# Two attention heads normed and turned together, a denser modulation vector and a longer queue of queries and keys

## The chip, the core and the metric

The kernel runs on one core of a Trainium2 chip. TensorE (PE, the matrix engine, with its weight loads shown as PEld), VectorE (DVE), ScalarE (ACT) and GpSimd (POOL) each work through a queue of their own, in order; SyncE (SP) issues most DMAs. Semaphores tie the queues together. The metric is the device time of one execution in microseconds (us); lower is better. Shown are the median of several runs and one execution taken apart by the profiler.

## The reference

One layer: adaptive modulation of a normed input, a projection `w_in`, sparse attention and an RWKV time mix side by side, an output projection, and a gated feed-forward network (FFN), all in float32 on 512 tokens of width 2048.

```python
mod = silu(c) @ w_ada[l] + b_ada[l]
sh1, sc1, gt1, sh2, sc2, gt2 = jnp.split(mod[:, None, :], 6, axis=-1)
h = rms_norm(x, norm1_g[l]) * (1 + sc1) + sh1
proj = h @ w_in[l]                    # q, k, v, iq, ik, iw and the RWKV columns
q = partial_rope(rms_norm(q.reshape(B, S, 8, 128), q_norm_g[l]), positions)
k = partial_rope(rms_norm(k.reshape(B, S, 8, 128), k_norm_g[l]), positions)
att_out = dsa_sparse_attention(q, k, v, iq, ik, iw)   # each query keeps its 128 best keys
rwkv_out = rwkv7_time_mix(rwkv_proj, ...)
x = x + gt1 * (jnp.concatenate([att_out, rwkv_out], axis=-1) @ w_out[l])
h2 = rms_norm(x, norm2_g[l]) * (1 + sc2) + sh2
x = x + gt2 * ((silu(h2 @ w_ffn_gate[l]) * (h2 @ w_ffn_up[l])) @ w_ffn_down[l])
```

`partial_rope` turns the first 32 of a head's 128 columns. In the kernel a head lies as a tile of 128 columns (partitions) by 512 tokens, so the turned part is its first 32 partitions.

## The kernel before

**Dense work.** All projections are *jobs* of weights: a job is a chunk of four 128-row blocks of a weight matrix times 256 columns. Each float32 operand is split into a high and a low part (`split`: the high part by an ACT cast, `whi`; the low by a DVE subtraction, `wlo`), and each product is three matmuls, so a chunk gives 24 matmuls of 128x128 by 512, and a pair of heads, four chunks, 96. Weights come through four DMA buffers (`wraw`) and four buffers each of `whi` and `wlo`, one for half a chunk. A pair of heads gathers in two of four `pg` banks of PSUM, and `evac_qk` empties them on ACT: for each head `t` (the head times its gain, named `q` or `k` in the trace) and a square `sq`.

**Side work.** Everything else runs as *streams*: Python generators that `drive` steps after every three matmuls (`every=3` in `run_jobs`). The program is written out once, by a planner that keeps a clock for each engine (`clk`, `cost`, `ready`): a stream waits with `until` (its inputs ready by the planner's clock), `room` (DVE's clock at most so far ahead of PE's) and `banks` (a free PSUM bank), and then writes its instructions into the queues between the matmuls. Where a job's `need` is not met, no matmul is written; the planner's clock moves on in steps of 0.25 until it is. On the chip only the order in each queue and the semaphores are left of that.

**Around the change.** The attention jobs come in the order q0 and q1, k0 and k1, q2 and q3, k2 and k3, and so on, each with `need=few`. `qk` holds heads whose `q` or `k` is made and not yet taken by `head`; two `head_stream`s take them once the top-k of the index scores (`idx_stream`: 16 rounds of `max` and `match_replace` on DVE) is done and both RWKV `scan`s are through (`scanned`). `scan` is a chain of eight steps, each of short matmuls (tiles `p`, `po`) with copies between; then `post` norms the RWKV heads (`pm`, `pst`, `prb`, `pgt`). `norm_qk`, one stream for each head, takes the column sums (`colsum`: a DVE transpose into `tr` and a sum into `sums`), turns the head in place (`rope`: a shuffle and three DVE operations on 32 rows, temporary `u`), spreads the sums by short matmuls into `pst`, takes the power -1/2 on POOL into `rr`, and for a key lays it out with four transposes (`prb`) and multiplies (DVE). Most of these tiles, and those of the heads (`lt`, `vh`), of `post` (`bv`, `sq`) and of the modulation vectors (`wad`), come from one pool `gp` of 27 tiles; an instruction that needs a tile waits until one is given back. Among jobs after the q/k groups are the output projection (`wout`, needs the ended heads) and the FFN.

`ada_stream` makes the modulation vectors `gt1`, `sh2`, `sc2`, `gt2`: 64 chunks each, loaded by SP (`wad`, 256 KB) and multiplied and added on DVE, one chunk at a time at a pace of `PACE1`, `PACE`, `PACE2`. `gt2` starts in the FFN; at its end `ada_sum` sums over partitions into `part`, then the short matmuls `pc`. All down projections have `need=lambda: done["ada"] == 16`, that is, `gt2` must be there.

In the profile nearly every instruction has line 127, the planner's helper, so groups are told apart by tile names.

Of the kernel before, what the change touches and what calls it, by code (L numbers as in the profile page):

```python
# [8 lines left out]
F32 = mybir.dt.float32  # L9
F32R = mybir.dt.float32r  # L10
I32 = mybir.dt.int32
AF = mybir.ActivationFunctionType
OP = mybir.AluOpType
# [6 lines left out]
NT = S // 128  # L20
# [6 lines left out]
NORM_EPS = 1e-6  # L27
# [16 lines left out]
C_FQ, C_FI, C_SQ, C_SI, C_HS, C_ONE, C_SEL, C_EXP, C_MOD = 512, 513, 514, 515, 516, 518, 519, 520, 522  # L44
# [4 lines left out]
def layer_kernel(ctx, tc, x, c, positions, w_ada, b_ada, norm1_g, w_in, q_norm_g, k_norm_g,  # L49
# [13 lines left out]
    def nm(ap):  # L63
        t = getattr(ap, "tensor", None)
        return getattr(t, "name", None)
# [22 lines left out]
    class Queue:  # L88
# [3 lines left out]
        def __getattr__(self, op):  # L92
# [3 lines left out]
            def call(*args, **kw):  # L96
# [26 lines left out]
                if key2 != "pe":  # L123
                    for v in vals[1:]:
                        if nm(v) in psread:
# [4 lines left out]
    PE, V, A, P, SP = (Queue(e, k) for e, k in ((nc.tensor, "pe"), (nc.vector, "dve"), (nc.scalar, "act"),  # L130
                                                (nc.gpsimd, "pool"), (nc.sync, "dma")))

    def now():
        return clk["pe"]

    SLACK = 0.5
    PACE1, PACE, PACE2 = 3.6, 1.9, 3.0

    def until(*aps):

        t = max(ready.get(nm(a), 0.0) for a in aps) + SLACK
        while now() < t:
            yield

    def room(key="dve", lim=3.0):
        while clk[key] - now() > lim:
            yield

    def banks(n):

        while True:
            for k in [k for k, v in psread.items() if v is not None and v <= now()]:
                del psread[k]
            if len(psread) + n <= 4 and side["pe"] <= SIDE:
                return
            yield
# [12 lines left out]
    rpool = ctx.enter_context(tc.tile_pool(name="rp", bufs=8))  # L169
# [3 lines left out]
    def G(name="g", dt=F32):  # L173
        return gpool.tile([128, 512], dt, name=name, tag="g")
# [7 lines left out]
    def SM(name="sm"):  # L182
        return spool.tile([128, 16], F32, name=name, tag="sm")
# [4 lines left out]
    def PS(name="ps"):  # L188
        t = psp.tile([128, 512], F32, name=name, tag="ps")
        psread[nm(t)] = None  # L190
        return t

    def mm(o, l, r, start=True, stop=True):
        PE.matmul(o, l, r, start=start, stop=stop)
# [8 lines left out]
    ident = cst[:, C_ID:C_ID + 128]  # L203
# [5 lines left out]
    mhalf = cst[:, C_EXP:C_EXP + 1]  # L209
# [148 lines left out]
    for k1, n1 in BLOCKS:  # L358
        for kind in ("scale", "shift"):
            n = 4 // n1  # L360
# [56 lines left out]
    ps = PS()  # L417
# [18 lines left out]
    att = {}  # L436
# [88 lines left out]
    def colsum(dst, t):  # L525

        u = G("tr")
        V.transpose(u, t)
        V.tensor_reduce(dst, u.rearrange("p (b c) -> p b c", c=32), axis=mybir.AxisListType.X, op=OP.add)

    def spread(ps, parts, col=C_MOD):

        pv = parts.rearrange("p (j a) -> p a j", a=4)
        for a in range(4):
            mm(ps[32 * a:32 * a + 32], cst[:, col:col + 32], pv[:, a, :])
# [294 lines left out]
    scanned = set()  # L830
# [142 lines left out]
    def ada_stream():  # L973
# [15 lines left out]
        for i, (bi, k) in enumerate(chunks):  # L989
            while (bi >= 12 and not state["ffn"]) or (4 <= bi < 12 and len(solved) < 2):  # L990
                yield
            while nl < min(i + 3, 64 if bi < 4 else 192 if bi < 12 else 256):
                load(nl)
                nl += 1
            t = tiles.pop(i)
            while now() < last + (PACE1 if bi < 4 else PACE if bi < 12 else PACE2):
                yield
            yield from until(t)
            yield from room("dve", 0.7 if 4 <= bi and not done["topk"] else 3.5)
            last = now()  # L1000
            if k == 0:
                A.activation(t, t, AF.Copy, scale=ccol(0))
                acc = t
                continue
            V.scalar_tensor_tensor(acc, t, ccol(k), acc, op0=OP.mult, op1=OP.add)
            if k == KD - 1:
                start(ada_sum(acc, *blocks[bi]))

    def ada_sum(acc, n, o, b):
        yield from until(acc)  # L1010
        part = parts[o % 2]
        yield from room("dve", 4.0)
        colsum(part[:, b * 16:b * 16 + 16], acc)
        if b < 3:
            return
        yield from until(part)
        t = now()
        while n == "gt2" and now() < t + 12.0:
            yield
        yield from banks(1)  # L1020
        pc = PS("pc")
        spread(pc[:, 0:16], part)
        yield
        V.tensor_tensor(mod[n], pc[:, 0:16], v1[:, o * 16:o * 16 + 16], op=OP.add)
        if n == "sc2":
            V.scalar_tensor_tensor(gp2, mod[n], 1.0, v1[:, 112:128], op0=OP.add, op1=OP.mult)
        done["ada"] += 4
# [3 lines left out]
    QM = [(i + 16) % 32 for i in range(32)]  # L1031
    IM = [i ^ 8 if i < 16 else i for i in range(32)]

    def rope(t, rows, tab, mask):
        cs, sn = tab
        u = G("u")
        V.stream_shuffle(u[rows], t[rows], mask)
        V.tensor_tensor(u[rows], u[rows], sn[rows], op=OP.mult)
        V.tensor_tensor(t[rows], t[rows], cs[rows], op=OP.mult)
        V.tensor_tensor(t[rows], t[rows], u[rows], op=OP.add)  # L1040
# [91 lines left out]
    head_queue = []  # L1132
    qk = {}
    qstat = {}

    def evac_qk(kind, i0):
        def f(ps):
            gcol = v2[:, R_QN:R_QN + 1] if kind == "q" else v2[:, R_KN:R_KN + 1]
            for i in range(2):
                t, sq = G(kind), G("sq" + kind)  # L1140
                A.activation(t, ps[i], AF.Identity, scale=gcol)
                A.activation(sq, ps[i], AF.Square)
                qk[kind, i0 + i] = t
                start(norm_qk(kind, i0 + i, t, sq))
        return f

    def norm_qk(kind, h, t, sq):
        yield from until(sq)
        yield from room()
        sm = SM("sums")  # L1150
        colsum(sm, sq)
        rope(t, slice(0, 32), att["qtab"], QM)
        yield from until(sm)
        yield from banks(1)
        pst = PS("pst")
        spread(pst[:, 0:4], sm)
        yield
        st, rr = SM("st"), rpool.tile([128, 4], F32, name="rr", tag="rr")
        V.tensor_scalar(st[:, 0:4], pst[:, 0:4], 1.0 / 128, NORM_EPS, op0=OP.mult, op1=OP.add)
        P.tensor_tensor(rr, st[:, 0:4], mhalf.broadcast_to([128, 4]), op=OP.pow)  # L1160
        if kind == "q":
            P.tensor_scalar(rr, rr, 128.0 ** -0.5, 0.0, op0=OP.mult, op1=OP.add)
            qstat[h] = rr
            return
        yield from until(rr)
        yield from banks(1)
        prb = PS("prb")
        for tt in range(NT):
            PE.transpose(prb[:, tt * 128:(tt + 1) * 128], rr[:, tt:tt + 1].broadcast_to([128, 128]), ident)
        yield  # L1170
        V.tensor_tensor(t, t, prb, op=OP.mult)
        head_queue.append(h)


    PLACE = {3: (0, 0), 2: (1, 0), 0: (1, 384), 1: (2, 0)}
# [67 lines left out]
    def start(gen):  # L1243
        streams.append(gen)
# [27 lines left out]
        done["hfree"] += 4  # L1272

    def few():
        return len(qk) <= (6 if len(scanned) == 2 else 4)

    for h in range(0, HEADS, 2):
        group_T(win, h * 128, TWO, ALLK, 4, hrhs, evac_qk("q", h), need=few)
        group_T(win, 1024 + h * 128, TWO, ALLK, 4, hrhs, evac_qk("k", h), need=few, chunk_done=h_free if h == HEADS - 2 else None)
# [253 lines left out]
def constants():  # L1533
    import numpy as np
    t = np.zeros((128, C_W), np.float32)
    p = np.arange(128)
    t[:, C_ID:C_ID + 128] = np.eye(128)
    s, u = p[:, None] % 64, p[None, :] % 64
    t[:, C_MASK:C_MASK + 128] = np.where(p[None, :] < 64, s < u, s <= u)
    t[:, C_CAUS:C_CAUS + 128] = np.where(p[None, :] <= p[:, None], 0.0, FILL)  # L1540
    t[:, C_BLKM:C_BLKM + 128] = (p[:, None] // 64 == p[None, :] // 64) / 64.0
    fq = (np.float32(500000.0) ** (-np.arange(16, dtype=np.float32) / np.float32(16))).astype(np.float32)
    fi = (np.float32(500000.0) ** (-np.arange(8, dtype=np.float32) / np.float32(8))).astype(np.float32)
    t[0:32, C_FQ] = fq[p[:32] % 16]
    r = p % 64
    t[:, C_FI] = np.where(r < 16, fi[p % 8], 0.0)
    t[0:32, C_SQ] = np.where(p[:32] < 16, -1.0, 1.0)
    t[:, C_SI] = np.where(r < 8, -1.0, np.where(r < 16, 1.0, 0.0))
    t[:, C_HS] = p < 64
    t[:, C_HS + 1] = p >= 64  # L1550
    t[:, C_ONE] = 1.0
    t[:, C_SEL] = p % 32 == 0
    t[:, C_EXP] = -0.5
    t[:, C_MOD:C_MOD + 32] = p[:, None] % 32 == np.arange(32)
    t[0:64, C_MOD + 32:C_MOD + 64] = t[0:64, C_MOD:C_MOD + 32]
    t[64:128, C_MOD + 64:C_MOD + 96] = t[64:128, C_MOD:C_MOD + 32]
    return t
# [30 lines left out]
```

## Time and profile before

| | |
|---|---|
| median of three runs | 2716.01 us (2714.59 to 2717.59) |
| the profiled execution | 2714.33 us, of it a span of 2712.5 us from first to last instruction |
| PE busy | 2649.6 us, 98% of the span |
| DVE busy | 1458.6 us, 54% |
| ACT busy | 807.6 us, 30% |
| POOL busy | 181.0 us, 7% |
| granted TensorE clock, mean | 0.987 of full speed |

A view of stretches gives busy time of each engine between two times from the span's start. A view of waits says what ended an engine's idle times. The chain of waits follows the work that ended last back in time. A granted clock of 1.00 is 2.4 GHz, 0.50 is 1.2 GHz; a value between is a mean over a stretch that has both.

### The profile page before, as it was taken

To read this page: it belongs to the slowest core of one execution; us is meant where nothing else is said; L and a number is where in the kernel's file an instruction comes from. 1 tells how busy PE (TensorE), PEld (TensorE's weight loads), DVE (VectorE), ACT (ScalarE), POOL (GpSimd) and SP (SyncE) were. 2 spreads that over 40 slices of the span, in tenths; PEclk is the share of its full clock that TensorE was granted. 3 is DMA by queue.
4 is the path that set the end of the run, shared out by engine and by line. 5 is a ranking of instruction groups with operands and counts; after the bars stand their busy time and mean duration, and the time that the engine had idled before them with its cause. 6 is when DMAs were issued, how large, how long until landed. Compare 5 with 4: busy or idle time off the path is not lost.

```text
span 2712.5 us, 35153 instructions
## 1 busy us (share of the span) xinstructions
PE 2649.6 (98%) x13351; PEld 2102.1 (77%) x13351; DVE 1458.6 (54%) x2542; ACT 807.6 (30%) x1475; POOL 181.0 (7%) x194
## 2 busy tenths in 40 slices
PE   7999999999998999999999899999999999999999
PEld 4477777767776787887888788888888888888887
DVE  3367779979788778755555432323333232332333
ACT  3243333323322334323322222222222222222222
POOL 2001101100021223110000000000000000000000
PEclk8999999999998999999999999999999999999999
DMA  9966675573664344752555232333233332323233
GB/s 323 335 215 194 215 192 179 163 192 115 173 206 126 125 156 144 250 173 64 197 170 177 95 101 94 101 94 97 98 97 98 96 99 95 100 94 101 93 104 98
DMA packets 383802, 396.10 MB, mean 146 GB/s; under 512 B 52538, under 2 KB 332928, under 8 KB 383632
## 3 DMA queue, kind: packets, MB, share of 16 engines
q1 hardware_dynamic: 381392, 387.25, 45.8%
q0 software_dynamic: 2096, 6.34, 0.7%
q8 instruction: 105, 1.72, 0.3%
q14 instruction: 65, 0.53, 0.1%
q10 hardware_dynamic: 144, 0.26, 0.0%
HBM read 358.13 MB, written 35.65 MB: 145 GB/s over the span
## 4 chain that ended last, share of the span: by engine, by line
PE 89%; DVE 5%; issue 2%; DMA 2%; SPq 1%; ACT 1%; POOL 0%; POOLq 0%; DVEq 0%; ACTq 0%
PE acc L127 75%; PE vacc L127 4%; PE p L127 2%; PE po L127 2%; SPq L127 1%; PE adaacc L127 1%; DVE wlo L127 1%; PE dot L127 1%; DVE stmp L127 1%; DMA wada<-in_w_ada_dram 1%; PE pl L127 1%; DVE wad L127 0%; PE pgt L127 0%; DMA xtok<-in_x_dram 0%; DVE X L127 0%
## 5 line engine op out<-in xcount | busy, mean ns | idle before, releaser
L127 DVE TENSOR_TENSOR wlo<-wraw,whi 128x512 fp32r<-128x512 f32 (+2 forms) x868 | 578.8, 673 | 1007.5 <-ACT whi L127 1003.2
L127 PE MATMUL acc<-hhi,whi 128*128 128x512 f32 (+1 forms) x2256 | 908.9, 403 | 6.6 <-ACT hhi L127 6.4
L127 ACT CAST whi<-wraw 128x512 fp32r<-128x512 f32 (+2 forms) x868 | 519.2, 604 | 1304.3 <-PE acc L127 1206.6
L127 PE MATMUL acc<-hhi,wlo 128*128 128x512 f32 (+1 forms) x2256 | 882.4, 391 | 1.6 <-DVE wlo L127 1.5
L127 PE MATMUL acc<-hlo,whi 128*128 128x512 f32 (+1 forms) x2256 | 882.3, 391 | 1.2 <-DVE hlo L127 1.1
L127 PEld LDWEIGHTS acc<-hhi,whi 128*128 128x128 f32 (+1 forms) x2256 | 423.6, 188 | 126.4 <-issue 28.6
L127 PEld LDWEIGHTS acc<-hhi,wlo 128*128 128x128 f32 (+1 forms) x2256 | 423.6, 188 | 94.2 <-DVE wlo L127 2.9
L127 PEld LDWEIGHTS acc<-hlo,whi 128*128 128x128 f32 (+1 forms) x2256 | 424.1, 188 | 92.2 <-issue 5.8
L127 PE MATMUL acc<-act,whi 128*128 128x512 f32 x1408 | 437.0, 392 | 0.0
L127 PEld LDWEIGHTS acc<-act,whi 128*128 128x128 f32 x1408 | 264.4, 189 | 54.3
L127 PE MATMUL acc<-act,wlo 128*128 128x512 f32 x704 | 275.0, 391 | 0.0
L127 DVE SCALAR_TENSOR_TENSOR wad<-wad,cact 128x512 f32<-128x512 f32 x240 | 185.1, 771 | 0.9
L127 PEld LDWEIGHTS acc<-act,wlo 128*128 128x128 f32 x704 | 132.7, 188 | 27.7
L127 PE MATMUL acc<-mhi,whi 128*128 128x512 f32 x256 | 100.4, 392 | 0.0
L127 PE MATMUL acc<-mhi,wlo 128*128 128x512 f32 x256 | 99.7, 389 | 0.0
L127 PE MATMUL acc<-mlo,whi 128*128 128x512 f32 x256 | 99.6, 389 | 0.0
L127 DVE SCALAR_TENSOR_TENSOR x<-acc,gt,x 128x512 f32<-128x512 f32 x80 | 57.2, 750 | 38.8 <-PE acc L127 38.8
L127 DVE TENSOR_TENSOR X<-X,stmp 128x462 f32<-128x462 f32 (+21 forms) x138 | 70.7, 512 | 4.9
L127 DVE TENSOR_TENSOR stmp<-X,N 128x462 f32<-128x462 f32 (+21 forms) x138 | 70.7, 512 | 3.4 <-DMA N<-nab 1.7
L127 PEld LDWEIGHTS acc<-mhi,wlo 128*128 128x128 f32 x256 | 48.0, 188 | 10.1
L127 POOL TENSOR_TENSOR rn<-st,cst 128x8 f32<-128x8 f32 x16 | 29.1, 1817 | 400.6 <-DVE st L127 387.6
L127 PEld LDWEIGHTS acc<-mlo,whi 128*128 128x128 f32 x256 | 48.1, 188 | 9.9
(253 smaller groups left out, 1985.7 us busy)
## 6 DMA issues: line engine op xcount, KB each, us to landing
wad<-in_w_ada_dram SPq DMA_DIRECT2D x256, 256.0 KB, 4.3
wraw<-in_w_in_dram SPq DMA_DIRECT2D x107, 512.0 KB, 5.0
wraw<-in_w_ffn_down_dram SPq DMA_DIRECT2D x88, 512.0 KB, 3.5
wraw<-in_w_ffn_up_dram SPq DMA_DIRECT2D x84, 512.0 KB, 3.5
wraw<-in_w_ffn_gate_dram SPq DMA_DIRECT2D x80, 512.0 KB, 3.5
wada<-in_w_ada_dram SPq DMA_DIRECT2D x128, 256.0 KB, 6.7
wraw<-in_w_out_dram SPq DMA_DIRECT2D x32, 512.0 KB, 3.6
pk<-pack SPq DMA_DIRECT2D x16, 768.0 KB, 4.4
```

The source lines that it names most:

```text
L127: return f(*args, **kw)
```

## The change

Three edits. The modulation vector `gt2` is queued at a pace of 2.0 in place of 3.0, and its sum no longer holds for 12 units of the planner's clock before `pc`. `norm_qk` runs once for a pair of heads: ACT writes the first 32 rows of both heads, times the gain, a second time, side by side into a tile `rt` of 64 rows; DVE turns those together, and ACT copies each half back into its head; sums and `pst` of both heads share one scaling on DVE and one power on POOL, 128x8 in place of twice 128x4. The constants of frequency and sign are laid out for 64 rows. And `few` lets six in place of four heads wait in `qk`, and eight in place of six once both scans are through.

```diff
-    PACE1, PACE, PACE2 = 3.6, 1.9, 3.0
+    PACE1, PACE, PACE2 = 3.6, 1.9, 2.0
@@ ada_sum
         yield from until(part)
-        t = now()
-        while n == "gt2" and now() < t + 12.0:
-            yield
         yield from banks(1)
@@ evac_qk
+            ts, sqs, rt = [], [], G("rt" + kind)
             for i in range(2):
                 t, sq = G(kind), G("sq" + kind)
                 A.activation(t, ps[i], AF.Identity, scale=gcol)
+                A.activation(rt[32 * i:32 * i + 32], ps[i][0:32], AF.Identity, scale=gcol[0:32])
                 A.activation(sq, ps[i], AF.Square)
                 qk[kind, i0 + i] = t
-                start(norm_qk(kind, i0 + i, t, sq))
+                ts.append(t)
+                sqs.append(sq)
+            start(norm_qk(kind, i0, ts, sqs, rt))
@@ norm_qk
-    def norm_qk(kind, h, t, sq):
-        yield from until(sq)
+    def norm_qk(kind, h0, ts, sqs, rt):
+
+        yield from until(*sqs)
         yield from room()
-        sm = SM("sums")
-        colsum(sm, sq)
-        rope(t, slice(0, 32), att["qtab"], QM)
-        yield from until(sm)
+        sm = []
+        for sq in sqs:
+            sm.append(SM("sums"))
+            colsum(sm[-1], sq)
+        rope(rt, slice(0, 64), att["qtab"], QM)
+        for i, t in enumerate(ts):
+            A.copy(t[0:32], rt[32 * i:32 * i + 32])
+        yield from until(*sm)
         yield from banks(1)
         pst = PS("pst")
-        spread(pst[:, 0:4], sm)
+        for i in range(2):
+            spread(pst[:, 4 * i:4 * i + 4], sm[i])
         yield
-        st, rr = SM("st"), rpool.tile([128, 4], F32, name="rr", tag="rr")
+        st, rr = SM("st"), rpool.tile([128, 8], F32, name="rr", tag="rr")
...
-        yield from until(rr)
-        yield from banks(1)
-        prb = PS("prb")
-        for tt in range(NT):
-            PE.transpose(prb[:, tt * 128:(tt + 1) * 128], rr[:, tt:tt + 1].broadcast_to([128, 128]), ident)
-        yield
-        V.tensor_tensor(t, t, prb, op=OP.mult)
-        head_queue.append(h)
+        yield from until(rr, *ts)
+        for i, t in enumerate(ts):
+            yield from banks(1)
+            prb = PS("prb")
+            for tt in range(NT):
+                PE.transpose(prb[:, tt * 128:(tt + 1) * 128], rr[:, 4 * i + tt:4 * i + tt + 1].broadcast_to([128, 128]), ident)
+            yield
+            V.tensor_tensor(t, t, prb, op=OP.mult)
+            head_queue.append(h0 + i)
@@ few
-        return len(qk) <= (6 if len(scanned) == 2 else 4)
+        return len(qk) <= (8 if len(scanned) == 2 else 6)
```

## Rows read from the trace of the kernel before

**Rows 1.** busy time by stretch: PE, PEld, DVE, ACT, POOL, clock, DMA, GB/s.

```profile
850.00:890.00 40.00, 29.95 (x207) 23.21 (x206) 33.25 (x75) 7.97 (x16) 3.51 (x5) 0.74 0.34 106
1100.00:1200.00 100.00, 100.00 (x450) 82.53 (x449) 72.09 (x102) 29.70 (x49) 12.97 (x9) 1.00 0.68 230
1310.00:1510.00 200.00, 200.00 (x884) 165.58 (x884) 104.51 (x158) 61.65 (x103) 0.00 (x0) 1.00 0.54 180
1510.00:1530.00 20.00, 12.75 (x52) 10.06 (x51) 10.11 (x16) 3.00 (x5) 0.00 (x0) 0.74 0.17 52
```

**Rows 2.** what PE waited for, 700 to 1110: us in total, times, longest.

```profile
PE pst L127 <- DVE sums L127: 3.8, 1, 3.8
PE p L127 <- issue: 3.5, 1, 3.5
PE prb L127 <- POOL rr L127: 3.4, 2, 2.2
PE acc L127 <- DVE wlo L127: 1.5, 1, 1.5
```

**Rows 3.** chain of waits, 844 to 909: start us, us, what.

```profile
844.02 2.52 PE po L127 x24
...
850.99 1.95 PE p L127 x24
...
871.02 3.66 PE p L127 x24
...
878.92 3.60 PE po L127 x22
...
882.97 3.46 PE pm L127 x4
...
906.97 1.72 PE pm L127 x4
```

**Rows 4.** what PE waited for, 1110 to 1600.

```profile
PE pc L127 <- DVE part L127: 7.3, 1, 7.3
```

**Rows 5.** chain of waits, two dense stretches.

```profile
1095.65 102.72 PE acc L127 x453
...
1522.22 27.96 PE acc L127 x111
```

**Rows 6.** the `wad` instructions in a stretch: us, DVE, ACT, clock, DMA share, GB/s.

```profile
1320.00:1400.00 80.00, 18.57 (x25) 0.72 (x1) 1.00 0.56 189
```

**Rows 7.** groups of instructions, DVE, rotation: busy us, mean ns, then idle before.

```profile
L127 DVE STREAM_SHUFFLE u<-iq 128x512 f32<-128x512 f32 x8 | 5.8, 727 | 0.0
...
L127 DVE STREAM_SHUFFLE u<-q 32x512 f32<-32x512 f32 x8 | 5.7, 716 | 0.0
...
L127 DVE TENSOR_TENSOR q<-q,u 32x512 f32<-32x512 f32 x8 | 5.4, 679 | 0.3
```

**Rows 8.** groups of instructions, POOL, 690 to 1110.

```profile
L127 POOL TENSOR_TENSOR rr<-st,cst 128x4 f32<-128x4 f32 x16 | 33.8, 2117 | 108.3 <-DVE st L127 108.1
...
L127 POOL TENSOR_TENSOR rn<-st,cst 128x8 f32<-128x8 f32 x8 | 14.0, 1745 | 58.2 <-DVE st L127 45.2 <-DMA wad<-in_w_ada_dram 13.0
```

**Rows 9.** groups of instructions, ACT, 690 to 1110, idle before and its releasers.

```profile
L127 ACT CAST whi<-wraw 128x512 fp32r<-128x512 f32 x88 | 54.4, 621 | 117.6 <-PE acc L127 90.6 <-issue 6.2 <-DMA ch<-pk 6.0
...
L127 ACT ACTIVATE k<-acc,v 128x512 f32<-128x512 f32 x8 | 5.5, 686 | 8.3 <-PE prb L127 3.6 <-PE acc L127 2.8 <-DVE wad L127 1.9
...
L127 ACT COPY attout<-po 128x512 f32<-128x512 f32 x8 | 4.7, 586 | 19.7 <-PE po L127 19.7
```

**Rows 10.** timeline of ACT at one evacuation: start us, us, what.

```profile
927.16 0.60 ACT L127 ACTIVATE sqk<-acc 128x512 f32<-128x512 f32 x1 [1.49 <-PE prb L127]
```

**Rows 11.** chain of waits at the heads' ends and starts.

```profile
950.26 4.46 PE po L127 x40
...
984.20 2.23 PE po L127 x20
...
1015.09 2.16 PE pl L127 x8
```

More of the change, by code (lines that the diff above doesn't have):

```diff
@@ L1154, in norm_qk @@
         yield from banks(1)
         pst = PS("pst")
-        spread(pst[:, 0:4], sm)
+        for i in range(2):
+            spread(pst[:, 4 * i:4 * i + 4], sm[i])
         yield
-        st, rr = SM("st"), rpool.tile([128, 4], F32, name="rr", tag="rr")
-        V.tensor_scalar(st[:, 0:4], pst[:, 0:4], 1.0 / 128, NORM_EPS, op0=OP.mult, op1=OP.add)
-        P.tensor_tensor(rr, st[:, 0:4], mhalf.broadcast_to([128, 4]), op=OP.pow)
+        st, rr = SM("st"), rpool.tile([128, 8], F32, name="rr", tag="rr")
@@ L1161, in norm_qk @@
+        V.tensor_scalar(st[:, 0:8], pst[:, 0:8], 1.0 / 128, NORM_EPS, op0=OP.mult, op1=OP.add)
+        P.tensor_tensor(rr, st[:, 0:8], mhalf.broadcast_to([128, 8]), op=OP.pow)
         if kind == "q":
             P.tensor_scalar(rr, rr, 128.0 ** -0.5, 0.0, op0=OP.mult, op1=OP.add)
-            qstat[h] = rr
+            for i in range(2):
+                qstat[h0 + i] = rr[:, 4 * i:4 * i + 4]
             return
-        yield from until(rr)
-        yield from banks(1)
-        prb = PS("prb")
@@ L1543, in constants @@
     fi = (np.float32(500000.0) ** (-np.arange(8, dtype=np.float32) / np.float32(8))).astype(np.float32)
-    t[0:32, C_FQ] = fq[p[:32] % 16]
+    t[0:64, C_FQ] = fq[p[:64] % 16]
     r = p % 64
     t[:, C_FI] = np.where(r < 16, fi[p % 8], 0.0)
-    t[0:32, C_SQ] = np.where(p[:32] < 16, -1.0, 1.0)
+    t[0:64, C_SQ] = np.where(p[:64] % 32 < 16, -1.0, 1.0)
     t[:, C_SI] = np.where(r < 8, -1.0, np.where(r < 16, 1.0, 0.0))
```

## The prediction

> **What bounds the kernel now.** I read the table of busy time by stretch first. The reader is to see that TensorE (PE) is the bound nearly everywhere: in a stretch such as 1310 to 1510 us it is busy for all of its 200 us while VectorE (DVE) is at half [rows 1]. A change to another engine is therefore worth only what it takes off PE's idle time, and off the time in which PE runs at the lower of its two clocks after idling. Two stretches touched by this change have both: 850 to 890 (busy 29.95 of 40 us, granted clock 0.74) and 1510 to 1530 (12.75 of 20, also 0.74) [rows 1]. Then I read PE's own waits, which name what ended each gap, and last the chain of waits, which shows what one and the same group of matmuls costs on either side of a gap.
>
> **Gap one, 850 to 890.** The queries q2, q3 are the last dense work that may be issued there: after them four query and two key tiles wait (six), so `few` (at most four until both scans are through) holds back k2, k3. What is left is the end of the second scan, a chain of short matmuls with copies between. PE waits for a norm sum 3.8 us, then 3.5 us ahead of the scan's next product without a releaser that the profile names, and for smaller things [rows 2]; idle in all 40 - 29.95 = 10.05 us [rows 1]. After it the clock is low: the scan's first product takes 3.66 us where the same 24 matmuls took 1.95, its output 3.60 against 2.52, the mean of a head pair 3.46 against 1.72 [rows 3]: 1.71 + 1.08 + 1.74 = 4.5 us lost to the clock, and the scan's middle product, without a row of its own there, some 0.8 by the same ratio (an estimate). Together 15.4 us.
>
> **Gap two, 1510 to 1530.** The first down projection may not be issued before `gt2` is summed, and in the stream of PE its sum `pc` stands right behind the last up matmul. PE waits 7.3 us for the vector `part` [rows 4], and the stretch's idle time is 20 - 12.75 = 7.25 us [rows 1]. The next 111 dense matmuls take 27.96 us; at 102.72/453 = 0.2268 us each they would take 25.17 [rows 5], so the low clock costs another 2.8. Together 10.0 us.
>
> **The change, part by part.**
>
> *Denser `gt2` (PACE2 3.0 to 2.0, no hold of 12).* The kernel's planner looks at the streams after every three matmuls, which it books at 3 x (512/2400 + 0.003) = 0.649 us. A pace of 3.0 is five such looks, 2.0 is four (three are 1.947, just short). In real matmuls that is 15 against 12, or 3.40 against 2.72 us; the trace has 25 chunks in 80 us, 3.2 each [rows 6]. So 64 chunks end 64 x (3.2 - 2.72) = 31 us earlier at least, and 7.3 are wanted: the whole gap of 10.0 us goes, and next to be late is nothing I can find, as down projections need only gate tiles long finished. The hold costs the planner idle time alone. What moves with it: 64 loads of 256 KB on SP's queue ahead of weight loads, and 64 multiply-adds on DVE, in a shorter time. From 1100 to 1200 the vectors are already queued at pace 1.9, DVE is busy 72 of 100 us and DMA 0.68, and PE is never idle [rows 1], so I cost this at nothing; if that cover failed, one late `wlo` costs 1.5 us [rows 2]. **-10.0.**
>
> *Six (later eight) tiles.* k2, k3 may now run in gap one: 96 matmuls x 0.2268 = 21.8 us of dense work [rows 5] for a hole of 15.4. They are covered by weights already split. DVE is the doubtful cover: 33.25 of 40 us busy there [rows 1]; eight more `wlo` come in at about 0.68 each (5.4, an estimate by the `q<-q,u` row of the same operation [rows 7]) and 2.8 go with one rotation (below), so it is just full, and the top-k rounds, which are queued only into room, yield. I credit -15.4 and keep -10 as the weak end.
>
> The other groups were not held back by `few`: heads take four tiles away each time before the next group asks. They all simply run some 15 us earlier.
>
> *Pairs.* Per query or key pair one rotation on 64 rows replaces two on 32: shuffle 0.716, two multiplies and an add of 0.68 each [rows 7], 2.76 us; eight pairs save 22 us of DVE. The shuffle of 128 rows takes 0.727 [rows 7], so 64 rows cost no more than 32. This lies beside PE; it shows only where PE waits for DVE or for what follows: the stall of 3.8 for sums, counted in gap one, and 3.4 for `prb` [rows 2]. Credit -1, between 0 and -3.4.
>
> POOL's power of -1/2 halves from 16 to 8 instructions in the stage. Four columns take 2.1 us on the mean, eight columns (in `rn`) 1.7 [rows 8]: no dearer. It is on PE's path only in those 3.4 us. Cost 0, between -3.4 and +3.4.
>
> ScalarE (ACT) gets per pair two scaled copies out of PSUM (0.686, as the `k` row) and two copies of 32 rows back (0.586, as `attout`) [rows 9]: 2.5 us, eight times 20. Its busy share has room for it. But the copies back are a **new wait** in ACT's queue, behind which the weights' `whi` casts stand, and PE waits for those. The wait ends when the rotation does: up to two sums and one rotation of DVE work. Casts are made as soon as one of four buffers is free (90.6 of the 117.6 us that ACT idles before `whi` are waits for PE [rows 9]), so they run three half-jobs of 12 matmuls ahead, 3 x 2.72 = 8.2 us. DVE's two transposes and two sums, at the shuffle's 0.7 each (an estimate), and a rotation are 2.8 + 2.76 = 5.6, plus up to 3 that the planner lets DVE lag, plus 1.2 for the copies: 9.8 at worst, 1.6 over the lead. So 0 to 1.6 for each of eight pairs, 0 to +13; none below nothing, as it only delays. I take +1, near the lower end, since before the `wlo` behind the cast stood behind two rotations anyway.
>
> *Buffers.* Pool `gp` has 27 tiles. At the evacuation of k2, k3 ACT already stood waiting for a tile: 3.6 us for `prb` to let go of a square and 1.9 for a `wad` [rows 9], until 927.16 [rows 10], and PE then lost 1.5 for a late `wlo` [rows 2]. The change keeps two more keys and one `rt` at that point. Lower end 0 (the evacuation may fall before the heads take theirs); upper end that ACT waits until heads 0 and 1 are through, rival two. Nearest is the row of the present wait: I take twice its damage, so +3 more.
>
> Merging speaks against a sentence of the Trainium skill (Perfetto Trace Analysis, Optimizing Scalar/DVE Operations): where Vector or Scalar work leaves bubbles on other engines, breaking instructions up may let work finish sooner. Here that would mean that the first key of a pair is late. By it the sum would be 3 worse, as rival three works out from rows; the trace of before has only one-head norms and cannot decide it.
>
> Sum: -10.0 - 15.4 - 1 + 0 + 1 + 3 = -22.4. Against the profiled execution's 2714.33 that gives 2692; the median of the runs, 2716.01, is 1.7 above it, so **2694 us**.
>
> **Rivals.**
>
> *One: the gap only moves.* The q/k work is a fixed amount; spent early, it is missing when the last heads run, and PE idles there instead. Only gap two is gained: 2716 - 10 = 2706, less if the clock stays up. It needs heads to be the bound. Against it: heads 2, 3 end at 984.20 + 2.23, heads 4, 5 begin at 1015.09 [rows 11]; for 28.7 us the heads wait for keys, and the keys are what comes earlier. For it: DVE is full in gap one, and top-k, for which all heads wait, may end later. Chance 0.15.
>
> *Two: slower.* The three extra tiles find no buffer, and ACT stays blocked at one evacuation from 927.16 [rows 10] until heads 0 and 1 give back theirs at 950.26 + 4.46 [rows 11], 27.6 us more, with `whi` behind it. PE's lead is used up by then, so nearly all is PE idle, and a restart costs 3 to 5 us of low clock as in both gaps: -25 + 27.6 + 4 = +6, 2722. It decides from about 22 us of extra blocking on. Against it: the queries' norm sets two squares free without ACT. Chance 0.06.
>
> *Three: pairing is late.* Both keys now wait for both sums: one transpose and one sum more on DVE, some 1.4 us, on the path where `prb` is waited for today (twice, 3.4 us [rows 2]), so +3 at most: 2697. Chance 0.07.
>
> *Four: the change doesn't do what it says at gap one*, because both scans are through only after k2, k3 and the next group stands still at eight tiles. Then some 5 of the 15.4 come back: 2699. Chance 0.07.
>
> **How the numbers follow.** Forecast 0.65: 2694, its own range 2687 to 2701 by the ends above. With rival one and the costs' upper ends the range reaches to 2709; below, the two costs of +4 may not come and the 4.9 us that PE waits for `prb` and `wlo` [rows 2] may go too: 2685. Rival two lies outside. A measurement can tell 0.2%, 5.4 us: faster means under 2710.6. Forecast, three and four are faster, of rival one 0.09 of 0.15: 0.88. Same 0.06 (the rest of rival one). Slower: rival two, 0.06.
>
> **What would show it.** Right: after 850 no stretch of 20 us up to 1100 with the clock under 0.9; dense `acc` matmuls between the scan's last products; PE's wait for `part` before `pc` gone and the last `gt2` chunk 30 us or more before the first down projection; DVE some 22 us less busy, ACT 20 more. Wrong: ACT's idle time before `q`, `k` or `rt` grows beyond 10 us with PE waiting for `wlo` (rival two); PE waits of 10 us or more near the last heads (rival one); ACT waiting for `rt` with PE short of `whi` (the new wait mis-sized).

## The result and the profile after

| | before | after |
|---|---|---|
| median of the runs | 2715.30 us (2713.30 to 2717.59, 6 runs) | 2698.69 us (2697.70 to 2700.07, 6 runs) |
| the profiled execution | 2714.33 us, span 2712.5 | 2699.81 us, span 2697.8 |
| DVE busy / ACT busy / POOL busy | 1458.6 / 807.6 / 181.0 us | 1437.8 / 825.1 / 161.7 us |

The changed kernel takes 0.9939 of the time before (95% interval 0.9928 to 0.9950), 16.6 us less by the medians; forecast were 2694 us, 22 less. Of the spans, 14.7 us apart, 4.7 lie ahead of the second norm (it begins at 1248.5 before and 1243.8 after) and 10.0 behind it. The page's line of busy times, of after:

```profile
PE 2645.0 (98%) x13351; PEld 2096.9 (78%) x13351; DVE 1437.8 (53%) x2494; ACT 825.1 (31%) x1507; POOL 161.7 (6%) x182
```

Busy time by stretch, after, with the columns of [rows 1]:

```profile
850.00:890.00 40.00, 40.00 (x281) 31.53 (x279) 29.02 (x61) 13.50 (x25) 2.83 (x3) 1.00 0.34 107
890.00:910.00 20.00, 15.29 (x72) 9.85 (x72) 15.06 (x30) 6.54 (x11) 5.03 (x4) 0.85 0.15 46
...
1040.00:1060.00 20.00, 12.75 (x60) 9.33 (x59) 15.39 (x26) 8.88 (x17) 2.21 (x2) 0.74 0.50 166
1280.00:1600.00 320.00, 320.00 (x1420) 264.81 (x1419) 156.75 (x243) 95.20 (x165) 0.00 (x0) 1.00 0.47 154
...
1510.00:1530.00 20.00, 20.00 (x90) 16.58 (x89) 8.53 (x14) 6.03 (x10) 0.00 (x0) 1.00 0.28 90
```

Both gaps of [rows 1] are closed: PE is busy for all of 850 to 890 and of 1510 to 1530, at clock 1.00. But two new holes stand at 890 to 910 (4.7 us idle) and at 1040 to 1060 (7.25 idle), where before both stretches were full:

```profile
890.00:910.00 20.00, 20.00 (x91) 14.82 (x90) 17.90 (x37) 3.40 (x6) 4.92 (x4) 1.00 0.37 115
1040.00:1060.00 20.00, 20.00 (x122) 16.48 (x121) 18.46 (x32) 12.12 (x22) 8.54 (x4) 1.00 0.55 185
```

What PE waited for from 690 to 1110 in after, and below it two rows of what ACT waited for:

```profile
PE acc L127 <- ACT mhi L127: 7.2, 1, 7.2
PE pgt L127 <- issue: 4.7, 1, 4.7
PE pt L127 <- POOL lt L127: 1.4, 3, 0.6
```

```profile
ACT q L127 <- DVE rtq L127: 28.7, 4, 8.1
ACT k L127 <- DVE rtk L127: 28.1, 4, 7.6
```

The chain of waits, after, shows both holes and the end of the heads:

```profile
897.09 1.72 PE pgt L127 x4
...
900.81 4.70 issue
905.51 3.75 PE pgt L127 x4
...
1003.10 2.16 PE pl L127 x8
...
1050.08 0.63 ACT k L127
1050.72 0.62 ACT k L127
1051.88 0.62 ACT mhi L127
1052.55 0.80 PE acc L127
...
1054.91 7.65 PE acc L127 x27
...
1086.21 4.47 PE po L127 x40
```

At 900.81 PE stands before the matmuls `pgt`. The profile names no releaser ("issue"); by the kernel they need a PSUM bank, and DVE sets one free by reading `prb`, which it does only after a whole pair's norm. That read ends at 905.41, and PE goes on at 905.51. DVE's timeline of that moment (start, duration, what, idle time before it):

```profile
898.11 0.69 DVE L127 TENSOR_TENSOR wlo<-wraw,whi 128x512 fp32r<-128x512 f32 x1 [3.29 <-ACT whi L127]
898.72 0.74 DVE L127 SCALAR_TENSOR_TENSOR wad<-wad,cact 128x512 f32<-128x512 f32 x1
899.38 0.70 DVE L127 STREAM_TRANSPOSE tr<-sqk 128x512 f32<-128x512 f32 x1
...
904.13 0.68 DVE L127 TENSOR_TENSOR rtk<-rtk,u 64x512 f32<-64x512 f32 x1
904.74 0.67 DVE L127 TENSOR_TENSOR O<-O,prb 128x512 f32<-128x512 f32 x1
```

At 1045 it is the new wait: ACT stands 7.57 us before the copies `k<-rtk` of the last keys, which begin at 1050.08. The casts `mhi` for the output projection are queued behind them, and PE runs dry.

**Where gap one's 15 us went** is read from five moments. The groups of after show for each the shortest, median and longest time in ns and the starts of the first and last instruction: the end of the top-k, the evacuation of the last key, the casts of the RWKV heads for the output projection (`mhi<-O`), the copy of the last head's output, and the second norm (`hx`).

```profile
L127 DVE TENSOR_SCALAR score<-score x3: 294/353/421, 934.1 to 934.6; 128x256 f32<-128x256 f32 x1, 128x384 f32<-128x384 f32 x1, 128x512 f32<-128x512 f32 x1
...
L127 ACT ACTIVATE k<-acc,v x8: 660/666/692, 822.0 to 1039.5; 128x512 f32<-128x512 f32 x8
...
L127 ACT CAST mhi<-O x8: 613/616/637, 1032.4 to 1052.9; 128x512 fp32r<-128x512 f32 x8
...
L127 ACT COPY attout<-po x8: 583/588/602, 961.2 to 1090.7; 128x512 f32<-128x512 f32 x8
...
L127 DVE SCALAR_TENSOR_TENSOR hx<-x,gp,prb x16: 737/740/747, 1243.8 to 1298.4; 128x512 f32<-128x512 f32 x16
```

The same rows of the other kernels of this study, in us, each from one profiled execution, which lies up to 3.1 us from the median of its kernel ("tail": from the last key to the last head; "by": how long before the last key the last `mhi<-O` begins, negative if after it):

| kernel | top-k ends | last key | last `mhi<-O` | by | last head | tail | second norm | median |
|---|---|---|---|---|---|---|---|---|
| before | 900.8 | 1053.1 | 1051.0 | 2.1 | 1095.7 | 42.6 | 1248.5 | 2715.3 |
| e1_pace | 901.6 | 1054.0 | 1051.9 | 2.1 | 1096.6 | 42.6 | 1249.4 | 2705.2 |
| e2_few | 942.7 | 1042.7 | 1051.2 | -8.5 | 1093.7 | 51.0 | 1247.8 | 2715.5 |
| e3_pair | 897.8 | 1046.0 | 1059.4 | -13.4 | 1097.2 | 51.2 | 1250.0 | 2718.0 |
| e6_pace_few | 943.2 | 1043.2 | 1051.7 | -8.5 | 1094.0 | 50.8 | 1246.5 | 2705.2 |
| **after** | 934.6 | 1039.5 | 1052.9 | -13.4 | 1090.7 | 51.2 | 1243.8 | 2698.7 |
| e4_late_copy | 916.5 | 1045.3 | 1054.8 | -9.5 | 1096.0 | 50.7 | 1249.0 | 2703.1 |
| e5_dve_add | 921.5 | 1037.5 | 1045.0 | -7.5 | 1084.5 | 47.0 | 1237.5 | 2696.7 |
| e7_break | 941.3 | 1040.8 | 1054.3 | -13.5 | 1091.0 | 50.2 | 1245.0 | 2698.9 |
| e8_topk_narrow | 933.3 | 1038.5 | 1051.9 | -13.4 | 1089.7 | 51.2 | 1242.7 | 2698.9 |
| e10_late_last | 934.8 | 1039.7 | 1045.5 | -5.8 | 1089.4 | 49.7 | 1243.4 | 2698.5 |
| e11_split_first | 901.0 | 1033.5 | 1023.1 | 10.4 | 1078.4 | 44.9 | 1230.9 | 2689.7 |
| e14_few_split_first | 929.0 | 1039.6 | 1034.1 | 5.5 | 1080.5 | 40.9 | 1233.4 | 2687.1 |
| e17_split_first_four | 894.7 | 1051.9 | 1052.9 | -1.0 | 1101.7 | 49.8 | 1254.3 | 2710.0 |

In every kernel the second norm begins 152.5 to 154.1 us after the last head. So the stage's end is the last key plus the tail. The change brings the last key 13.6 us forward, and the tail grows by 8.6: 5.0 are left.

What either part is made of shows in PE's busy time from 850 to the last key and from there to the last head, first before, then after:

```profile
850.00:1053.10 203.10, 189.22 (x1051) 150.47 (x1050) 160.28 (x333) 70.74 (x153) 51.16 (x49) 0.95 0.42 135
1053.10:1095.70 42.60, 40.26 (x226) 32.20 (x225) 36.75 (x74) 17.25 (x41) 15.65 (x10) 1.00 0.56 186
...
850.00:1039.50 189.50, 184.78 (x1053) 146.58 (x1052) 138.92 (x291) 79.15 (x168) 40.18 (x40) 0.98 0.42 133
1039.50:1090.70 51.20, 42.55 (x225) 33.20 (x224) 37.89 (x74) 21.74 (x48) 9.78 (x11) 0.90 0.50 162
```

PE has as many matmuls in each part as before. So the 8.6 us of the tail are 6.3 more of idle time and 2.3 of the same matmuls at a lower clock (0.90 for 1.00), and the 13.6 ahead of it are 9.2 less of idle time and 4.4 less for matmuls at a low clock (0.98 for 0.95 on the mean). Over both, idle time falls only from 16.2 to 13.4 us: what gap one gave back, the two new holes took. The same sum is 16.2 in e1, 16.4 in e2, 16.6 in e6, 4.9 in e11 and 3.3 in e14. Keys that come early don't by themselves leave PE short at the end: in e14 the last key comes when it does in after, and the tail is 40.9.

### The profile page after: what moved, and what is told of

Read it like the earlier page. It is cut to its first block, busy times and chain, and to the rows that moved or that the text cites. A ratio compares the mean times of both kernels' runs of the same rounds, so it can differ in the third digit from the quotient of the medians.

```text
span 2697.8 us, 35126 instructions
## 1 busy us (share of the span) xinstructions
PE 2645.0 (98%) x13351; PEld 2096.9 (78%) x13351; DVE 1437.8 (53%) x2494; ACT 825.1 (31%) x1507; POOL 161.7 (6%) x182
## 3 DMA queue, kind: packets, MB, share of 16 engines
q8 instruction: 105, 1.72, 0.3%
## 4 chain that ended last, share of the span: by engine, by line
PE 90%; DVE 4%; issue 2%; DMA 2%; SPq 1%; ACT 1%; POOL 0%; POOLq 0%; DVEq 0%; ACTq 0%
PE acc L127 77%; PE vacc L127 4%; PE p L127 2%; PE po L127 2%; PE adaacc L127 1%; DVE wlo L127 1%; DMA wada<-in_w_ada_dram 1%; SPq L127 1%; DVE stmp L127 1%; PE dot L127 1%; PE pl L127 1%; PE pgt L127 1%; DVE X L127 0%; PE pA L127 0%; DMA xtok<-in_x_dram 0%
## 5 line engine op out<-in xcount | busy, mean ns | idle before, releaser
L127 PEld LDWEIGHTS acc<-mhi,whi 128*128 128x128 f32 x256 | 48.6, 190 | 17.6 <-ACT mhi L127 7.7
L127 PEld LDWEIGHTS acc<-mlo,whi 128*128 128x128 f32 x256 | 48.5, 189 | 10.4 <-DVE mlo L127 0.5
```

The costliest lines, as they stand in the source:

```text
L127: return f(*args, **kw)
```

## The experiments

Each kernel's time is the median of its runs; ratios are to the kernel before on the same chip. A change of order in the program makes the planner lay out all that follows anew, except in e8_topk_narrow, whose queues keep their order.

### Each part alone

**e1_pace**: before, with `PACE2` 2.0 and without the hold.

```diff
-    PACE1, PACE, PACE2 = 3.6, 1.9, 3.0
+    PACE1, PACE, PACE2 = 3.6, 1.9, 2.0
...
-        t = now()
-        while n == "gt2" and now() < t + 12.0:
-            yield
```

> The kernel before with the denser pace of gt2 and without its hold alone. Theory: gap two (7.25 us idle and 2.8 us of low clock) goes and nothing else moves: 10 us off, 2705. Rival: the denser chunks collide with weight loads or with DVE's wlo, and a part comes back: 2709 or more, with new waits of PE for wlo between 1300 and 1500.

Measured: 2705.22 us, ratio 0.9964 (0.9951 to 0.9976), 10 us faster, as its theory said. `gt2` is made at 1484.0, 38.3 us earlier than before (1522.3), and PE no longer waits for it.

**e2_few**: before, with the longer queue alone.

```diff
-        return len(qk) <= (6 if len(scanned) == 2 else 4)
+        return len(qk) <= (8 if len(scanned) == 2 else 6)
```

> The kernel before with six (later eight) waiting tiles alone, heads still normed one by one. Theory A (the hole of gap one is filled, and what came back in the changed kernel is due to the pairs): 12 to 15 us off, 2700 to 2703, and no wait of 7 us for mhi. Theory B (the hole only moves to where the last heads run): at most 5 us off, 2710 or more, with PE waiting near 1050 to 1100 for mhi or for heads.

Measured: 2715.46 us, ratio 1.0001 (0.9992 to 1.0010): nothing. The last key comes 10.4 us earlier, the top-k ends 42 us later, the tail is 8.4 longer. PE's waits:

```profile
PE pst L127 <- DVE sums L127: 7.5, 2, 3.8
PE acc L127 <- DVE mlo L127: 4.5, 1, 4.5
```

The gap has moved: PE is idle as long as before in all, 8.5 us ahead of the last key (the two waits for sums, at 931 to 939, just before the heads) and 7.9 behind it. Theory B held.

**e3_pair**: before, with the paired norm alone: the hunks `evac_qk`, `norm_qk` and the constants of the change's diff, of which the core is

```diff
-                start(norm_qk(kind, i0 + i, t, sq))
+            start(norm_qk(kind, i0, ts, sqs, rt))
...
-        rope(t, slice(0, 32), att["qtab"], QM)
+        rope(rt, slice(0, 64), att["qtab"], QM)
+        for i, t in enumerate(ts):
+            A.copy(t[0:32], rt[32 * i:32 * i + 32])
```

> The kernel before with heads normed and turned in pairs alone; pace and limits as before. Theory A (ACT's copies back make it wait for the rotation, with whi and mhi casts behind): 0 to 10 us slower, 2715 to 2725, depending on where the wait of ACT falls, with ACT waiting some 50 us in all for rtq and rtk. Theory B (DVE's 22 us less are worth more): 1 to 4 us faster, 2711 to 2714.

Measured: 2718.01 us, ratio 1.0009 (1.0000 to 1.0018). The last key comes 7.1 us earlier, and the tail is 8.6 longer; PE waits 7.2 us for `mhi` behind the copies, as in after. ACT waits 59.3 us in all for `rtq` and `rtk`. Theory A held, at the low end of its price, and pairing alone gains nothing.

**e6_pace_few**: before, with e1's and e2's edits and no pairs.

```diff
-    PACE1, PACE, PACE2 = 3.6, 1.9, 3.0
+    PACE1, PACE, PACE2 = 3.6, 1.9, 2.0
...
-        return len(qk) <= (6 if len(scanned) == 2 else 4)
+        return len(qk) <= (8 if len(scanned) == 2 else 6)
```

> The kernel before with the denser gt2 and the longer queue of heads, its norm still one head at a time. Theory A (each part is worth what it was worth alone: pace -10, queue 0): 2705, second norm at 1247 to 1249. Theory B (the queue pays only beside something that takes work off DVE, so that the pairs are what makes it pay): also 2705, and the changed kernel's further 6 us are the pairs' doing. Rival C (the queue pays beside the denser gt2, the pairs are worth nothing): 2698 to 2700.

Measured: 2705.18 us, ratio 0.9966 (0.9954 to 0.9978), the same as e1. So pace and queue add up to -10 and 0, and rival C falls. The changed kernel's further 6.5 us (3.2 between the profiled executions) come from pairs and queue together, though neither gives anything alone.

### The new wait on ACT

**e4_late_copy**: after, with ACT's copies queued only once the rotation is due.

```diff
         rope(rt, slice(0, 64), att["qtab"], QM)
+        yield from until(rt)
         for i, t in enumerate(ts):
```

> The changed kernel, but the copies back are written into ACT's queue only when the rotation should be done by the planner's clock, so ACT has the same work but does not stand waiting for it. Theory A (the wait in ACT's queue cost the 7.2 us at the last key pair and 2.6 us of low clock after it): 8 to 10 us under the changed kernel, 2689 to 2691, ACT's waits for rtq and rtk under 15 us in all. Theory B (PE stood there because dense work was missing): within 2 us of the changed kernel, 2697 to 2700, and the idle time of PE near 1050 is only put down to another wait.

Measured: 2703.12 us, ratio 0.9955 (0.9942 to 0.9968), 4.4 us slower than after by the medians, though the intervals overlap; the time lies outside both theories. ACT's waits for `rtq` and `rtk` fall from 56.8 us to 3.3, but the last key comes 5.8 us later, PE waits 6.6 us for `pst` at another place, and the tail stays. The wait removed is not the time gained.

**e10_late_last**: the same for the last pair of keys alone.

```diff
+        if kind == "k" and h0 == 6:
+            yield from until(rt)
         for i, t in enumerate(ts):
```

> The changed kernel, but for the last pair of keys alone ACT's two copies back are queued once the rotation is due, behind the casts of the output projection. All is the same up to 1040 us. Theory A (ACT's wait of 7.6 us there costs its 7.2 us of PE idle and some 4 us of low clock): the wait goes, 2690 to 2693. Theory B (another wait of the last heads takes its place): 2696 to 2700.

Measured: 2698.49 us, ratio 0.9939 (0.9927 to 0.9952), no gain. The 7.2 us for `mhi` are gone, and the low part of the same operand, behind the norm on DVE, takes the place:

```profile
PE acc L127 <- DVE mlo L127: 5.7, 1, 5.7
```

**e5_dve_add**: after, with the rotation's last addition made on DVE for each head and no copies.

```diff
-        rope(rt, slice(0, 64), att["qtab"], QM)
-        for i, t in enumerate(ts):
-            A.copy(t[0:32], rt[32 * i:32 * i + 32])
+        cs, sn = att["qtab"]
+        u = G("u")
+        V.stream_shuffle(u[0:64], rt[0:64], QM)
+        V.tensor_tensor(u[0:64], u[0:64], sn[0:64], op=OP.mult)
+        V.tensor_tensor(rt[0:64], rt[0:64], cs[0:64], op=OP.mult)
+        for i, t in enumerate(ts):
+            V.tensor_tensor(t[0:32], rt[32 * i:32 * i + 32], u[32 * i:32 * i + 32], op=OP.add)
```

> The changed kernel, but the rotation's last addition is made on DVE, one for each head straight into the head, in place of one addition on the pair and two copies on ACT. ACT then waits for no rotation; DVE has one addition of 0.68 us more for each of eight pairs, 5.4 us in all. Theory A (ACT's wait at the last keys, 7.2 us of PE idle and a restart at the low clock, is a price of the pairing): that wait goes, the last head ends some 8 us earlier, 2688 to 2692. Theory B (the last heads are set by their own chain, and PE would wait there for something else): 2696 to 2701.

Measured: 2696.74 us, ratio 0.9932 (0.9919 to 0.9944); the interval covers after's 0.9939. The tail is 47.0, and PE waits 5.2 us for `mlo` in place of 7.2 for `mhi`. In all three runs PE's wait for `mhi` goes and one for `mlo` comes (2.2 us in e4): ACT's wait was first in a line, and DVE's own part of the operands stands right behind it. Theory B held in e10 and e5.

### DVE: its load or its order

**e8_topk_narrow**: after, with the top-k's `max` and `match_replace` on 128 columns (the selection over the others is left out), booked by the planner at full width.

```diff
-                V.max(m8[:, 0:8], sc)
-                V.match_replace(sc, m8[:, 0:8], sc, TAKEN)
+                V.max(m8[:, 0:8], sc[:, 0:128])
+                V.match_replace(sc[:, 0:128], m8[:, 0:8], sc[:, 0:128], TAKEN)
```

> The changed kernel with every queue in the same order, but the top-k rounds look at the first 128 scores of a row only (the selection over the other columns is left out), while the plan books them as before: some 0.5 us less DVE work for each of 48 rounds. Theory A (once the hole is filled, DVE is the bound from 850 to 930): the new hole between 900 and 910 (4.7 us idle, then a low clock) closes, 2690 to 2693, and the second norm begins at 1236 to 1239. Theory B (PE waits there for something that DVE's load does not set): the hole stays, 2697 to 2700.

Measured: 2698.86 us, ratio 0.9941 (0.9928 to 0.9953). DVE's busy time from 850 to 890 falls from 29.02 to 24.27 us, yet the hole is as long as it was. Its stretch, a piece of its chain, and DVE's timeline ahead of the hole:

```profile
890.00:910.00 20.00, 15.29 (x69) 9.76 (x69) 15.04 (x32) 6.94 (x12) 4.46 (x4) 0.83 0.19 53
```

```profile
899.82 4.70 issue
904.53 3.75 PE pgt L127 x4
```

```profile
897.12 0.69 DVE L127 TENSOR_TENSOR wlo<-wraw,whi 128x512 fp32r<-128x512 f32 x1 [4.09 <-ACT whi L127]
```

Of what DVE gained some is spent idle here: 4.09 us in place of 3.29 before a `wlo` whose `whi` stands on ACT behind the evacuation of the keys. Then comes the norm, and only then what PE waits for. So it isn't the load of the top-k that leaves the hole; theory A, and with it the prediction's DVE that is "just full", fell. The norm itself, from 898.39 to 903.75, was not made lighter; the next run breaks it up.

**e7_break**: after, with a `yield` behind each head's column sum, so that other streams may queue work in between.

```diff
             colsum(sm[-1], sq)
+            yield
```

> The changed kernel, but the pair's norm is broken up on DVE: after each head's column sum the other streams get a turn before the next part is queued. Theory A (the order of the splits is what leaves the hole): 2696 to 2701. Theory B (the length of the pair's norm in one piece does): the hole at 900 to 905 shrinks by 2 to 4 us, and so does the wait at the last keys, 2690 to 2695; by the Trainium skill too (Perfetto Trace Analysis, Optimizing Scalar/DVE Operations), which lets instructions be broken up where they leave bubbles on other engines, this is the faster one.

Measured: 2698.93 us, ratio 0.9941 (0.9929 to 0.9954), as after. Theory A held. The hole goes from its place and comes back: 890 to 910 is full, but from 900 to 950 PE is idle 4.84 us (4.72 in after), now mostly for sums.

```profile
890.00:910.00 20.00, 20.00 (x92) 15.17 (x91) 11.54 (x24) 8.36 (x14) 4.49 (x4) 1.00 0.06 20
```

```profile
PE acc L127 <- ACT mhi L127: 7.3, 1, 7.3
PE pst L127 <- DVE sums L127: 4.2, 2, 3.1
```

The sentence of the Trainium skill on breaking up instructions (Perfetto Trace Analysis, Optimizing Scalar/DVE Operations) speaks of engines that aren't saturated, a condition that the prediction left out. e7 breaks up a sequence and not a single instruction; taken in that sense, the trace agrees for the bubble at 900 (4.7 us idle from 890 to 910, then none) and the run doesn't for the time (2698.93 for 2698.69).

### The order of the splits

**e11_split_first**: after; at the end of each group of queries or keys one more half chunk of weights is split ahead of the evacuation.

```diff
             if j["after"] is not None:
+                if j["view"] is win and j["c0"] < COL_V:
+                    split_to(j["s0"] + 6)
                 j["after"]()
```

> The changed kernel, but at the end of each group of queries or keys the split of one more half chunk of weights is queued ahead of the evacuation and not behind it: ACT makes whi before its six instructions on q, rt and sq, so DVE's wlo no longer holds up DVE until they are through. Theory A (what is left of the hole is the order in ACT's and DVE's queues: DVE stood idle 4 us before a wlo although its load was a third lower in the run with the narrow top-k, and then did the pair's norm ahead of what PE waited for): the hole of 4.7 us at 900 to 905 goes, heads 0 and 1 begin some 10 us earlier, second norm at 1234 to 1239, time 2688 to 2693. Theory B (the holes are set by how long the pair's norm takes on DVE, 5.5 us in one piece): no hole shrinks by more than 1 us, 2696 to 2701.

Measured: 2689.72 us, ratio 0.9905 (0.9891 to 0.9918), 9.0 us faster than after. ACT's timeline shows a cast directly ahead of the keys. One more stands behind them at 897.64, as the one at 897.47 in after, so ACT is one half chunk further; it isn't rid of the cast behind the evacuation. The two stretches of the holes are full:

```profile
893.61 0.62 ACT L127 CAST whi<-wraw 128x512 fp32r<-128x512 f32 x1 [3.48 <-PE acc L127]
894.14 0.68 ACT L127 ACTIVATE k<-acc,v 128x512 f32<-128x512 f32 x1
```

```profile
890.00:910.00 20.00, 20.00 (x94) 15.52 (x93) 16.96 (x36) 7.64 (x14) 5.04 (x4) 1.00 0.42 121
1040.00:1060.00 20.00, 20.00 (x116) 16.27 (x115) 17.66 (x31) 8.89 (x16) 2.01 (x1) 1.00 0.66 227
```

The top-k ends at 901.0 in place of 934.6, and the last `mhi<-O` begins 10.4 us ahead of the last key. Of the gain of 12.3 us at the last head (the profiled executions are 12.8 apart, the medians 9.0), 6.0 are the last key's and 6.3 the tail's. ACT still waits for the rotation (8.62 us before a `k<-rtk` at 906.88); PE, with another half chunk ready, is busy all through it. Theory A held.

**e14_few_split_first**: the same edit, on e6_pace_few, so without pairs (below with e6's longer queue, without its pace).

```diff
+                if j["view"] is win and j["c0"] < COL_V:
+                    split_to(j["s0"] + 6)
                 j["after"]()
...
-        return len(qk) <= (6 if len(scanned) == 2 else 4)
+        return len(qk) <= (8 if len(scanned) == 2 else 6)
```

> The kernel before with the denser gt2 and the longer queue, its norm still one head at a time, and the split of one more half chunk ahead of each evacuation of queries or keys. Beside the same without the earlier split (2705.2) this tells whether the queue's gain was lost to the order of the splits in the unpaired kernel too. Theory A: yes, the waits of 7.5 us for sums and 4.5 us for mlo shrink, 2694 to 2700. Theory B (DVE's 22 us more of rotation are what loses it there): 2702 to 2706.

Measured: 2687.06 us, ratio 0.9894 (0.9879 to 0.9909): 18 us faster than e6, and as fast as e11 or faster. It beats both kernels, with the old norm, and theory A (2694 to 2700) by 7. The 22 us of DVE time that pairs save are worth nothing here.

**e17_split_first_four**: the same, on e1_pace, so with the short queue and without pairs.

```diff
+                if j["view"] is win and j["c0"] < COL_V:
+                    split_to(j["s0"] + 6)
                 j["after"]()
```

> The kernel before with the denser gt2 and the split of one more half chunk ahead of each evacuation of queries or keys, but with the old queue of four and six tiles and no pairs. Theory A (the longer queue does fill gap one for 15 us, and the order of the splits only let it be lost later): the hole of 10 us at 850 to 890 stays, 2700 to 2705, against 2687.1 with the longer queue. Theory B (the order of the splits alone gives the 18 us, and the queue adds nothing): 2686 to 2690. In between, some part of each.

Measured: 2710.04 us, ratio 0.9979 (0.9970 to 0.9988). The early split alone is 4.8 us slower than e1 by the medians (the intervals touch). Gap one is there as before:

```profile
850.00:890.00 40.00, 30.38 (x199) 23.59 (x198) 34.95 (x78) 7.47 (x15) 3.01 (x5) 0.66 0.37 110
```

Four unpaired kernels, all with the denser `gt2`, thus make a table of two by two:

| | split behind the evacuation | split ahead of it |
|---|---|---|
| queue of 4 and 6 | 2705.2 (e1) | 2710.0 (e17) |
| queue of 6 and 8 | 2705.2 (e6) | 2687.1 (e14) |

The longer queue is worth 0 in the one order and 23.0 us in the other. Theory A's mechanism held: the hole stays, and what the queue fills is kept to the end only beside the early split. Its time (2700 to 2705) was missed, as it had not foreseen that the early split, without the queue, costs time. The cost isn't idle time: from 850 to the last head PE idles 16.4 us (16.2 in e1), but its matmuls, 1278 for 1281, take 4.9 us longer, at clock 0.66 for 0.74 from 850 to 890 and 0.93 for 1.00 in the tail.

## Why the prediction was right, and where it was not

The time, 2698.7 us, lies 4.7 above the forecast and within its range (2685 to 2709), and the likeliest case is the one that came, with one large term cut down. That it lies so near is in part luck: between the profiled executions 14.7 us came of 22.4, since gap one gave 10.7 less than forecast and a charge of 3 for buffers, which didn't come due, made up for some of it.

**Gap two: right.** -10.0 was forecast; e1 alone gives 10.0, and the spans are 10.0 apart behind the second norm. The wait for `part` [rows 4] is gone, and 64 denser chunks cost nothing: PE is busy for all of 1280 to 1600.

**Gap one: the mechanism was right, the term mis-sized.** k2, k3 run in the hole, which is filled at clock 1.00; nothing of 850 to 890 is left to gain. (One of its terms is a little low: for the scan's output it sets 3.60 us of 22 matmuls against 2.52 of 24 [rows 3].) Of -15.4 (weak end -10) 4.7 came at the second norm. The step that failed is that time saved at 850 lasts until the end of the stage. In its place two new holes came, of 4.7 and 7.2 us and a low clock behind each: 13.6 last until the last key, 8.6 are given back in the tail. This is rival one, "the gap only moves", in good part: for it the prediction had named a later top-k (934.6 for 900.8), and that came; against it, that heads wait for keys, which was true of heads 4, 5 (1015.09 before [rows 11], 1003.10 after), but not of the end. e2 shows rival one pure: no gain at all. But its reason, that work spent early must be missing later, isn't borne out: e14 spends it as early, and PE idles 3.3 us from 850 to the last head. The sign that the prediction set, no stretch of 20 us with the clock under 0.9 from 850 to 1100, was broken twice: 0.85 at 890 to 910, 0.74 at 1040 to 1060.

**Pairs: -1 was forecast for PE, with DVE 22 us less busy and POOL no dearer.** DVE's total fell by 20.8 us. The power on eight columns took on the mean as long as that on four [rows 8]:

```profile
L127 POOL TENSOR_TENSOR rr<-st,cst 128x8 f32<-128x8 f32 x8 | 17.4, 2176 | 114.5 <-DVE st L127 114.5
```

But what pairs are worth depends on what is beside them: +2.8 alone (e3, where the interval begins at no change), -6.5 with the longer queue (e6 to after), +2.7 with the early split (e14 to e11, where the intervals overlap). No one number for the part fits all three.

**ACT's new wait: seen, and mis-sized by place.** Forecast were 0 to 1.6 us for each of eight pairs. Seven waits of up to 8.1 us cost PE nothing that the profile names; one, at the last keys, costs 7.2, since `mhi` and not only `whi` stands behind it, and the lead of three half-jobs was reckoned for `whi` alone. Yet its net price is about zero: without it `mlo` is late (e10, e5).

**Buffers: +3 was forecast, 0 came.** ACT's waits for a free tile before `k` [rows 9] are gone; what is left is a wait for PE:

```profile
L127 ACT ACTIVATE k<-acc,v 128x512 f32<-128x512 f32 x8 | 5.4, 673 | 3.2 <-PE acc L127 3.2
```

So the forecast of -22.4 was -10.0 right, -15.4 for a gap that gave 4.7, and +3 for buffers that were free. Rival two needed that blocking, and it didn't come; rival three's late `prb` isn't among PE's waits; of rival four nothing is seen, as the dense matmuls stand in the hole.

**What stays open.** In 14 kernels the tail is 41 to 45 us, with 1.5 to 4.4 us of PE idle in it, where the last `mhi<-O` begins before the last key, and 47 to 51, with 5.2 to 8.7 idle, where after it. No run changed that order alone, so that it is the cause is a reading, not a proof. Nor is it shown by itself which link of e11 and e14 does most (the top-k's earlier end, the extra half chunk, the earlier `mhi`), since the edit makes the planner lay out everything after it anew; e14's top-k ends at 929.0, so that can't be all. Why pairs help beside the longer queue and not beside the early split was not taken apart, nor what lowers the clock in e17.

## What to carry to other kernels

A hole filled with work from later in the same stage is worth only what is left at the stage's end: follow the moment at which the filler would have run, and ask what the bounding engine does then. Edits that meet in one stage are to be tried two by two: here the longer queue is worth 0 or 23 us, depending on the place of a cast in another engine's in-order queue. Queuing such casts for the next matmuls ahead of an evacuation is worth a trial, beside whatever fills the holes: here it gave 9 and 18 us with the longer queue, and cost 4.8 without it. Whether an engine is full is tested by taking load off it with the order unchanged, before any work goes into lightening it.

## What the runs showed of the hardware that was not expected

The power on POOL took longer on more columns after all. Of the eight powers `rr` on 128x8 in the stage seven took 2.01 to 2.07 us, while the shortest on 128x4 before took 1.00, and the one at the second norm 1.02. Groups of `rr` and `rn` in after (shortest, median and longest in ns):

```profile
L127 POOL TENSOR_TENSOR rr<-st,cst x9: 1017/2011/3272, 807.5 to 1241.6; 128x8 f32<-128x8 f32 x8, 128x4 f32<-128x4 f32 x1
...
L127 POOL TENSOR_TENSOR rn<-st,cst x16: 1630/1704/2081, 212.3 to 920.3; 128x8 f32<-128x8 f32 x16
```

The mean of 2.1 us on four columns [rows 8], from which the prediction argued that eight are no dearer, is one of short and of long ones: before, they ran from 1.00 to 6.39 us. What makes them long was not tried, nor why `rn`, the same operation on as many columns, takes 1.63 at its shortest where `rr` takes 2.01. And after 4.70 us without a matmul at 900.81, four `pgt` took 3.75 us where four had taken 1.72 just before, so this hole cost some 2 us more than its idle time. The prediction had counted that for the old gaps and in rival two, and not for its new wait on ACT.
